# Skip weights on a diagonal per head, added by TensorE, in the scan of a hybrid backbone

## The chip, the cores and the metric

The kernel runs on one core of one Trainium2 chip. The metric is the device time of one launch in microseconds. Three timed runs and one profiled execution of the kernel before are shown below; clocks of TensorE are given as the granted share of full speed (1.00 is 2.4 GHz, 0.50 is 1.2 GHz).

## What is computed

The reference is one inference step of a small backbone: two layers, each applied to 128 context tokens and 1024 latent tokens. A layer norms its input, projects it, and sends parts of the projection to three mixers (attention, a bidirectional state space scan, a convolution module), joins their outputs in an output projection, and ends in a gated feed-forward block. The change is in the scan. Cut to what matters, the reference has:

```python
def ssd_mixer(comb, lp, h0):
    ...
    y = jnp.zeros_like(xs)
    for d in range(2):
        dt = jax.nn.softplus(dt_raw[:, :, d] + lp['ssd_dt_bias'][d])
        a = -jnp.exp(lp['ssd_a_log'][d])
        ...
        yd, hd = ssd_scan(*args, a, h0[:, d])
        ...
        y = y + yd + lp['ssd_d'][d][:, None] * xs
    y = rmsnorm(y.reshape(b, t, SSD_INNER) * jax.nn.silu(z), lp['ssd_norm_g'])
```

`xs` holds 4 heads of 64 values per token. `ssd_scan` works in chunks of 128 tokens: a product inside the chunk (with exponentials of the summed steps) and a product with the state that comes in. The term with `ssd_d` is the skip: each head's inputs times one weight, summed over both directions.

## The kernel before, in words

Tokens are in 9 chunks of 128 (chunk 0 is the context) and in 3 blocks of 384. A layer goes through these stages: projection of the scan's inputs; the mixer stage, where the scan, the projections of the convolution module and of the latents, and the latents' norms run beside each other; attention; output projection; feed-forward. Within the mixer stage generators are stepped through by a string of letters (line 735), so that projections stand between pieces of the scan; the framework then schedules the instructions: it sets the order of each engine's queue by readiness in its own model of the timing, so a change in one place moves neighbours too. Each queue runs strictly in the order thus set.

Values are split in two parts of fp32r ("hi" and "lo") and `mm3` (lines 100 to 105) makes three products of each pair. The projections of the latents from tokens (lines 592 to 614) have 416 columns; they are called projections here, and 24 of them make one tile of 128 tokens.

The scan's output is `ssd_out` (line 474). For a chunk c:

- W holds the step weights of both directions (4 ScalarE products L492, 4 VectorE steps L494), times the chunk's gram matrices (L497 on TensorE, L500 on VectorE).
- Masks for the exponents: for both directions and for hi and lo a tile `mv` of 512 columns, the hi ones by VectorE (L511), the lo ones by four ScalarE products (L509); TensorE multiplies each with a triangle of ones into one bank (L514). Three buffers of `mv`.
- E is the exponential of that (L516) times W (L517).
- TensorE multiplies E with the chunk's inputs, head by head, into `yb`, a bank of tag T (L523). There are eight banks in all: five of tag A, two of tag T, one of tag V.
- VectorE makes y: inputs times `dsum`, the summed skip weights (L525), plus `yb` (L527). From chunk 1 on, the state products of two groups (L532, banks of tag T too) are scaled into `of` (L534), and both directions of `of` are added to y (line 537; the helper's line is 78).
- z times y (L540), its squares summed by ScalarE (L541); every third chunk a norm (L545, L548).

The core of the sum, before:

```python
                y = tmp(256, "y", 2)
                V.tensor_tensor(y.rearrange("p (h q) -> p h q", h=4), xst[:, c].rearrange("p (h q) -> p h q", h=4),
                                dsum.unsqueeze(2).to_broadcast([128, 4, 64]), ALU.mult)
                V.tensor_add(y, y, yb[:, :256])
```

`token_tail` (line 620) norms three latent tiles (L639 to L646) and transposes them (L654, L661) into the latents, which VectorE splits (L581). After the last of these, `prep_r` (line 744) loads rope tables by SP into `tb` (L750) and multiplies them with products (L755); the first scores of attention follow. SP runs its loads in order; ahead of the tables in layer 0 it loads layer 1's rows of weights into a tile that the latents' norm has just read.

Of the kernel before, what the change touches and what calls it, by code (L numbers as in the profile page):

```python
# [9 lines left out]
F32R = mybir.dt.float32r  # L10
I32 = mybir.dt.int32
AF = mybir.ActivationFunctionType
ALU = mybir.AluOpType
# [40 lines left out]
def build(tc, nc, ap, dbg=None):  # L54
    V, S, G, PE, Q = nc.vector, nc.scalar, nc.gpsimd, nc.tensor, nc.sync
# [17 lines left out]
    def bank(tag):  # L73
        n = {"A": 5, "T": 2, "V": 1}[tag]
        return ps.tile([128, 512], F32, tag=tag, name="ps" + tag, bufs=n)

    def add_to(eng, out, a, b):
        eng.tensor_tensor(out, a, b, ALU.add)
# [4 lines left out]
    def copy(out, x):  # L83
        S.activation(out, x, AF.Copy)  # L84
# [47 lines left out]
    ident = cst[:, 0:128]  # L132
# [5 lines left out]
    def P(name, i):  # L138
        return par[:, PAR[name] + i:PAR[name] + i + 1]

    def small(w, tag, bufs=2):
        return sm.tile([128, w], F32, tag=tag, name=tag, bufs=bufs)

    def rsqrt(v, w):
        y = small(w, "ry")
        t = small(w, "rt")
        V.tensor_scalar(y.bitcast(I32), v.bitcast(I32), -0.5, RSQRT_MAGIC, ALU.mult, ALU.add)
        for _ in range(3):
            V.scalar_tensor_tensor(t, y, -0.5, y, ALU.mult, ALU.mult)
            V.tensor_mul(t, t, v)  # L150
            V.scalar_tensor_tensor(y, t, 1.5, y, ALU.add, ALU.mult)
        return y
# [157 lines left out]
    for l in range(L):  # L310
# [62 lines left out]
        def tmp(w, tag, bufs, dt=F32):  # L373
            return w1p.tile([128, w], dt, tag=tag, name=tag, bufs=bufs)


        tmp(512, "mv", 3, F32R)
        tmp(512, "E", 4)

        def xcol(t):  # L380
            return 128 * t + (XP if t else 0)
# [3 lines left out]
        def st_(name, w=72, dt=F32):  # L385
            return w1p.tile([128, w], dt, name=name)
# [20 lines left out]
        def v4(x):  # L407
            return x.rearrange("p (d c h) -> p d c h", d=2, c=9)
# [6 lines left out]
        for i, m in enumerate(M_in + M_st):  # L415
            d = i % 2
# [12 lines left out]
        xst = w1p.tile([128, 9, 256], F32, name="xst")  # L429
# [2 lines left out]
        Q.dma_start(Hin[:, 7, 1], ap["h0"][l, :, 128:256])  # L432
        dsum = st_("dsum", 4)
        V.tensor_add(dsum, rows[:, 16:20], rows[:, 20:24])
        ssz = st_("ssz", 9)


# [36 lines left out]
        def ssd_out():  # L474
            yz, late = [], None

            def tail():
                k, ys = late
                for j in range(2):
                    tb = bank("V")  # L480
                    for t in range(3):
                        PE.transpose(tb[:, 128 * t:128 * t + 128], ys[t][:, 128 * j:128 * j + 128], ident)
                    mo = tmp(CH, "sg", 2)
                    S.activation(mo, tb[:, :CH], AF.Copy, scale=P("ng", 2 * l + j))
                    S.dma_start(m_dram[k][4][:, j], mo)

            for c in range(9):
                o = xcol(c)

                W = tmp(512, "E", 4).rearrange("p (h t) -> p h t", h=4)  # L490
                for h in range(4):
                    S.activation(W[:, h], M_in[0], AF.Copy, scale=v4(dt)[:, 0, c, h:h + 1])  # L492
                for h in range(4):
                    V.scalar_tensor_tensor(W[:, h], M_in[1], v4(dt)[:, 1, c, h:h + 1], W[:, h], ALU.mult, ALU.add)  # L494
                gb = [bank("A"), bank("A")]
                for g in range(2):
                    PE.matmul(gb[g][:, :128], xc[2][64 * g:64 * g + 64, o:o + 128],  # L497
                              xc[3][64 * g:64 * g + 64, o:o + 128], start=True, stop=True)
                for g in range(2):
                    V.tensor_mul(W[:, 2 * g:2 * g + 2], W[:, 2 * g:2 * g + 2],  # L500
                                 gb[g][:, :128].unsqueeze(1).to_broadcast([128, 2, 128]))

                db = bank("A")
                for d in range(2):
                    for i, dd in enumerate((dah, dal)):
                        mv = tmp(512, "mv", 3, F32R).rearrange("p (h t) -> p h t", h=4)
                        if i:
                            for h in range(4):
                                S.activation(mv[:, h], M_in[d], AF.Copy, scale=v4(dd.bitcast(F32))[:, d, c, h:h + 1])  # L509
                        else:  # L510
                            V.tensor_tensor(mv, M_in[d].unsqueeze(1).to_broadcast([128, 4, 128]),  # L511
                                            v4(dd.bitcast(F32))[:, d, c, :].unsqueeze(2).to_broadcast([128, 4, 128]),
                                            ALU.mult)
                        PE.matmul(db, M_sr[d], mv.rearrange("p h t -> p (h t)"), start=d + i == 0, stop=d + i == 2)  # L514
                E = tmp(512, "E", 4).rearrange("p (h t) -> p h t", h=4)
                S.activation(E, db.rearrange("p (h t) -> p h t", h=4), AF.Exp)  # L516
                V.tensor_mul(E, E, W)  # L517
                if late:
                    tail()
                    late = None  # L520
                yb = bank("T")
                for h in range(4):
                    PE.matmul(yb[:, 64 * h:64 * h + 64], E[:, h], xst[:, c, 64 * h:64 * h + 64], start=True, stop=True)  # L523
                y = tmp(256, "y", 2)
                V.tensor_tensor(y.rearrange("p (h q) -> p h q", h=4), xst[:, c].rearrange("p (h q) -> p h q", h=4),  # L525
                                dsum.unsqueeze(2).to_broadcast([128, 4, 64]), ALU.mult)
                V.tensor_add(y, y, yb[:, :256])  # L527
                if c:
                    of = tmp(512, "of", 2).rearrange("p (d h q) -> p d h q", d=2, h=4)
                    for g in range(2):  # L530
                        ob = bank("T")
                        PE.matmul(ob[:, :256], xc[3][64 * g:64 * g + 64, o:o + 128],  # L532
                                  Hin[64 * g:64 * g + 64, c - 1].rearrange("p d n -> p (d n)"), start=True, stop=True)
                        V.tensor_mul(of[:, :, 2 * g:2 * g + 2], ob[:, :256].rearrange("p (d h q) -> p d h q", d=2, h=2),  # L534
                                     v4(ex[:, 0:72])[:, :, c, 2 * g:2 * g + 2].unsqueeze(3).to_broadcast([128, 2, 2, 64]))
                    for d in range(2):
                        add_to(V, y, of[:, d].rearrange("p h q -> p (h q)"), y)
                z = tmp(256, "zr", 4)
                Q.dma_start(z, z_dram[:, c])
                V.tensor_mul(z, z, y)  # L540
                S.activation(y, z, AF.Square, accum_out=ssz[:, c:c + 1])  # L541
                yz.append(z)
                if c % 3 == 2:
                    v = small(3, "nv")
                    V.tensor_scalar(v, ssz[:, c - 2:c + 1], 1.0 / 256, 1e-6, ALU.mult, ALU.add)  # L545
                    r = rsqrt(v, 3)
                    for t in range(3):
                        V.tensor_scalar_mul(yz[t], yz[t], r[:, t:t + 1])  # L548
                    late = (c // 3, yz)
                    yz = []  # L550
                yield
            tail()
# [116 lines left out]
        def step(g, n=1):  # L669
            for _ in range(n):  # L670
                next(g, None)

        st, cv, tm, so = ssd_states(), conv_in(), token_major(), ssd_out()
        gens = {"c": cv, "S": st, "t": tm, "o": so}

# [507 lines left out]
```

## Time and profile before

| | us |
|---|---|
| timed runs | 3262.02, 3253.57, 3265.45 |
| median of these | 3262.02 |
| profiled execution | 3262.04 |
| its span, first to last instruction | 3260.2 |
| busy: TensorE, VectorE, ScalarE, GpSimd | 3118.9, 1770.6, 1145.2, 1069.8 |
| mean granted clock of TensorE | 0.98 |

The mixer stage lies at about 143 to 308 us in layer 0 and 1768 to 1933 us in layer 1. How to read the rows: durations of products on TensorE overlap, so what one costs is the distance from its start to the next start; an arrow in brackets names the time an engine sat idle before an instruction and what ended that. fp32 products are recorded as two each.

### The profile page before, as it was taken

Reading aid. Unit: us, or ns where it says so; the run is one execution under the profiler, and the core shown is the slowest. Engines: PE = TensorE matmul, PEld = TensorE weight load, DVE = VectorE, ACT = ScalarE, POOL = GpSimd, SP = SyncE. Lnnn points to the kernel's source line nnn. Section 1 sums busy time; section 2 is a strip of 40 time slices with the busy share of each in tenths; the row PEclk is TensorE's granted clock in tenths of the full one; section 3 lists DMA queues with packets and bytes.
Section 4 is the critical chain, followed back from the end, with each engine's and each line's share of the span. In section 5 each row is a group of like instructions: output and inputs, shape, how many; then the busy total and the mean of one; then the engine's idle time right before and its main releaser. Section 6 shows DMA issues by size and latency. Waiting matters only on the chain. (4 is left out here: it accounts for less than half of the span.)

```text
span 3260.2 us, 50734 instructions
## 1 busy us (share of the span) xinstructions
PE 3118.9 (96%) x20610; PEld 2898.2 (89%) x20610; DVE 1770.6 (54%) x3891; ACT 1145.2 (35%) x2677; POOL 1069.8 (33%) x601
## 2 busy tenths in 40 slices
PE   7997998999999999999999989999999999999997
PEld 5986777779999999999999867777999999999997
DVE  6768777663633333333386688777373333334335
ACT  4465544562411111111144666566341111111113
POOL 2302998012511221112133039980242221122112
PEclk9998999999999999999999989999999999999998
DMA  6112333342111111111121010001301111111111
GB/s 237 49 31 86 116 118 104 124 171 80 49 42 40 40 51 40 39 40 39 52 103 55 24 58 9 13 6 50 143 27 52 39 52 40 39 42 50 39 33 59
DMA packets 67003, 202.38 MB, mean 62 GB/s; under 512 B 7888, under 2 KB 25424, under 8 KB 65232
## 3 DMA queue, kind: packets, MB, share of 16 engines
q1 hardware_dynamic: 63456, 194.02, 18.0%
q10 hardware_dynamic: 3312, 5.11, 0.4%
q8 instruction: 162, 2.65, 0.3%
q14 instruction: 73, 0.60, 0.1%
HBM read 177.44 MB, written 21.66 MB: 61 GB/s over the span
## 5 line engine op out<-in xcount | busy, mean ns | idle before, releaser
L81 POOL TENSOR_TENSOR wl<-ws,wh 128x1024 fp32r<-128x1024 f32 x164 | 396.0, 2421 | 1611.4 <-ACT wh L84 1571.9
L103 PE MATMUL psA<-hh,wh 128*128 128x384 f32 x2496 | 837.5, 337 | 4.3 <-ACT hh L270 2.7
L104 PE MATMUL psA<-hl,wh 128*128 128x384 f32 x2496 | 838.8, 337 | 1.4 <-DVE hl L267 0.8
L105 PE MATMUL psA<-hh,wl 128*128 128x384 f32 x2496 | 838.3, 336 | 0.0
L103 PEld LDWEIGHTS psA<-hh,wh 128*128 128x128 f32 x2496 | 471.4, 189 | 8.3 <-ACT hh L270 3.9
L104 PEld LDWEIGHTS psA<-hl,wh 128*128 128x128 f32 x2496 | 471.4, 189 | 4.7 <-DVE hl L267 1.7
L105 PEld LDWEIGHTS psA<-hh,wl 128*128 128x128 f32 x2496 | 471.1, 189 | 0.6
L1000 DVE TENSOR_TENSOR fs<-fs,psA 128x384 f32<-128x384 f32 x132 | 72.9, 554 | 666.3 <-PE psA L105 657.3
L873 POOL TENSOR_TENSOR acc<-ct,acc 128x1167 f32<-128x1167 f32 x120 | 326.3, 2719 | 10.0
L84 ACT ACTIVATE wh<-ws 128x1024 fp32r<-128x1024 f32 (+1 forms) x178 | 184.7, 1049 | 401.4 <-PE psA L104 196.3
L999 ACT ACTIVATE fs<-psA 128x384 f32<-128x384 f32 x132 | 63.9, 485 | 655.1 <-PE psA L105 655.0
L810 ACT ACTIVATE P<-psA,mx 128x384 f32<-128x384 f32 (+1 forms) x400 | 224.1, 570 | 128.2 <-DVE mx L808 88.0
L1053 DVE SCALAR_TENSOR_TENSOR x<-psT,mod,x 128x384 f32<-128x384 f32 (+1 forms) x320 | 157.8, 513 | 198.6 <-PE psT L105 198.6
L805 DVE TENSOR_REDUCE mx<-psA 128x1 f32<-128x384 f32 (+1 forms) x400 | 209.3, 540 | 76.5 <-PE psA L105 74.1
L1053 DVE SCALAR_TENSOR_TENSOR x<-psA,mod,x 128x384 f32<-128x384 f32 (+2 forms) x384 | 186.9, 513 | 53.3 <-PE psA L105 46.9
L1003 DVE TENSOR_TENSOR fl<-fs,fh 128x384 fp32r<-128x384 f32 x132 | 167.6, 1271 | 65.9 <-ACT fh L84 65.9
L842 PE MATMUL psV<-pt,vv 128*64 128x128 f32 x2336 | 192.8, 286 | 5.8 <-DVE pt L836 3.9
L831 PE MATMUL psT<-cst,P 128*128 128x128 f32 x1168 | 194.3, 288 | 2.8 <-ACT P L810 1.1
L104 PE MATMUL psA<-fl,wh 128*128 128x384 f32 x576 | 193.6, 336 | 0.0
L105 PE MATMUL psA<-fh,wl 128*128 128x384 f32 x576 | 193.5, 336 | 0.0
L103 PE MATMUL psA<-fh,wh 128*128 128x384 f32 x576 | 190.0, 337 | 2.7 <-DVE fs L1000 2.7
L103 PE MATMUL psA<-K,q 128*128 128x384 f32 (+1 forms) x400 | 159.9, 400 | 29.8 <-ACT P L810 23.7
(265 smaller groups left out, 5884.2 us busy)
## 6 DMA issues: line engine op xcount, KB each, us to landing
ws<-w_ada SPq DMA_DIRECT2D x96, 512.0 KB, 3.3
ws<-w_gate SPq DMA_DIRECT2D x44, 512.0 KB, 3.6
ws<-w_up SPq DMA_DIRECT2D x44, 512.0 KB, 3.6
ws<-w_down SPq DMA_DIRECT2D x44, 512.0 KB, 3.6
x<-xT SPq DMA_DIRECT2D x6, 1536.0 KB, 7.8
ws<-w_fm SPq DMA_DIRECT2D x16, 512.0 KB, 3.5
ws<-w_out SPq DMA_DIRECT2D x16, 512.0 KB, 3.7
mf<-mixed SPq DMA_DIRECT2D x18, 384.0 KB, 5.5
```

Source lines behind the costliest of these rows:

```text
L81: eng.tensor_tensor(out, x, hi.bitcast(F32), ALU.subtract)
L84: S.activation(out, x, AF.Copy)
L103: PE.matmul(out, sh, mh, start=i == 0, stop=False)
L104: PE.matmul(out, sh, ml, start=False, stop=False)
L105: PE.matmul(out, sl, mh, start=False, stop=i == n - 1)
L805: V.reduce_max(mx[:, b:b + 1], b0[:, :w], axis=AX.X)
L810: S.activation(pr[:, CH * b:CH * b + w], bs[b][:, :w], AF.Exp, bias=mx[:, 3:4], scale=SCALE, accum_out=sl[:, 3 * j + b:3 * j + b + 1])
L831: PE.transpose(tb[:, 256 * u + 128 * j:256 * u + 128 * j + 128], prs[j][:, 128 * (a + u):128 * (a + u) + 128], ident)
L842: PE.matmul(ob[64 * j:64 * j + 64, :128], vv[:, kt, 64 * h:64 * h + 64], pt[:, 256 * u + 128 * j:256 * u + 128 * j + 128], start=kt == kts ...
L873: last_tap[0] = G.tensor_tensor(acc[j][:, :CO], ct[:, :CO], acc[j][:, :CO], ALU.add)
L1003: V.tensor_sub(fl[:, sl], sg, fh[:, sl].bitcast(F32))
L1053: V.scalar_tensor_tensor(X[c][:, m, a:b], b0[:, a:b], modT[l][:, 40 + m, s:s + 1], X[c][:, m, a:b], ALU.mult, ALU.add)
```

## The change

Per layer, ScalarE writes four diagonal matrices `dI`, one per head: the identity times that head's summed skip weight. In each chunk TensorE multiplies `dI` with the chunk's inputs into the sum's bank first, and the product with E is added to it there. VectorE's product with `dsum` and the addition of the bank go; the bank is now added to the first direction of `of` (from chunk 1 on), the second direction follows, and in chunk 0 ScalarE copies the bank to y. The tile `mv` has two buffers instead of three; `dI` takes as much memory as one of them.

```diff
-        tmp(512, "mv", 3, F32R)
+        tmp(512, "mv", 2, F32R)
@@
         V.tensor_add(dsum, rows[:, 16:20], rows[:, 20:24])
+        dI = st_("dI", 512).rearrange("p (h t) -> p h t", h=4)
+        for h in range(4):
+            S.activation(dI[:, h], ident, AF.Copy, scale=dsum[:, h:h + 1])
@@
-                        mv = tmp(512, "mv", 3, F32R).rearrange("p (h t) -> p h t", h=4)
+                        mv = tmp(512, "mv", 2, F32R).rearrange("p (h t) -> p h t", h=4)
@@
                 yb = bank("T")
                 for h in range(4):
-                    PE.matmul(yb[:, 64 * h:64 * h + 64], E[:, h], xst[:, c, 64 * h:64 * h + 64], start=True, stop=True)
+                    xh = xst[:, c, 64 * h:64 * h + 64]
+                    PE.matmul(yb[:, 64 * h:64 * h + 64], dI[:, h], xh, start=True, stop=False)
+                    PE.matmul(yb[:, 64 * h:64 * h + 64], E[:, h], xh, start=False, stop=True)
                 y = tmp(256, "y", 2)
-                V.tensor_tensor(y.rearrange("p (h q) -> p h q", h=4), xst[:, c].rearrange("p (h q) -> p h q", h=4),
-                                dsum.unsqueeze(2).to_broadcast([128, 4, 64]), ALU.mult)
-                V.tensor_add(y, y, yb[:, :256])
@@
-                    for d in range(2):
-                        add_to(V, y, of[:, d].rearrange("p h q -> p (h q)"), y)
+                    V.tensor_add(y, of[:, 0].rearrange("p h q -> p (h q)"), yb[:, :256])
+                    add_to(V, y, of[:, 1].rearrange("p h q -> p (h q)"), y)
+                else:
+                    copy(y, yb[:, :256])
```

Lines move by 3 to 4 in the changed kernel: L497, L514, L517, L523 and L532 become L500, L517, L520, L528 and L534 on TensorE and VectorE, and L527 is now the product with `dI`.

The scheduler sets each engine's order anew. TensorE's queue in layer 0 from chunk 5's products with E (`psT<-xst,E`) to its state products (`psT<-Hin,raw_691`), before; `psA<-mv,gtlt` are exponent products, `psA<-raw_691,raw_690` gram products, `128x416` projections:

```order
L523 MATMUL psT<-xst,E 128x64 x4
L514 MATMUL psA<-mv,gtlt 128x512
L105 MATMUL psA<-wh,hl 128x416
L103 MATMUL psA<-wh,hh 128x416
L104 MATMUL psA<-wl,hh 128x416
L105 MATMUL psA<-wh,hl 128x416
L497 MATMUL psA<-raw_691,raw_690 128x128 x2
L514 MATMUL psA<-mv,gtlt 128x512 x2
L532 MATMUL psT<-Hin,raw_691 128x256 x2
```

The same place in the changed kernel, from the last head's two products on:

```order
L527 MATMUL psT<-xst,dI 128x64
L528 MATMUL psT<-xst,E 128x64
L517 MATMUL psA<-mv,gtlt 128x512
L500 MATMUL psA<-raw_691,raw_690 128x128 x2
L517 MATMUL psA<-mv,gtlt 128x512
L534 MATMUL psT<-Hin,raw_691 128x256
L103 MATMUL psA<-wh,hh 128x416
```

One state product now stands there, followed by 24 projections (the first is shown). The other one comes behind these:

```order
L105 MATMUL psA<-wh,hl 128x416
L534 MATMUL psT<-Hin,raw_691 128x256
L517 MATMUL psA<-mv,gtlt 128x512 x2
L103 MATMUL psA<-wh,hh 128x416
L104 MATMUL psA<-wl,hh 128x416
L105 MATMUL psA<-wh,hl 128x416
```

After it come two exponent products and 20 projections, and then chunk 6's products with `dI` and E. Counted from the stage's start, 309 of the three-part products (L103 to L105) stand ahead of chunk 5's products with E before, 313 now.

VectorE's queue at the same place, before (`psT,ex` is the scaling of a state product, `zr<-zr,y` the product with z that ends a chunk):

```order
L527 TENSOR_TENSOR y<-y,psT 128x256
L511 TENSOR_TENSOR mv<-cst,dah 128x512
L525 TENSOR_TENSOR y<-xst,dsum 128x256
L517 TENSOR_TENSOR E<-E 128x512
L494 SCALAR_TENSOR_TENSOR E<-cst,dt,E 128x128 x4
L534 TENSOR_TENSOR of<-psT,ex 128x2x128
L500 TENSOR_TENSOR E<-E,psA 128x256
L534 TENSOR_TENSOR of<-psT,ex 128x2x128
L500 TENSOR_TENSOR E<-E,psA 128x256
L78 TENSOR_TENSOR y<-of,y 128x256 x2
L540 TENSOR_TENSOR zr<-zr,y 128x256
```

And in the changed kernel:

```order
L514 TENSOR_TENSOR mv<-cst,dah 128x512
L520 TENSOR_TENSOR E<-E 128x512
L536 TENSOR_TENSOR of<-psT,ex 128x2x128
L497 SCALAR_TENSOR_TENSOR E<-cst,dt,E 128x128 x4
L503 TENSOR_TENSOR E<-E,psA 128x256 x2
L536 TENSOR_TENSOR of<-psT,ex 128x2x128
L538 TENSOR_TENSOR y<-of,psT 128x256
L78 TENSOR_TENSOR y<-of,y 128x256
L544 TENSOR_TENSOR zr<-zr,y 128x256
L81 TENSOR_TENSOR wl<-ws,wh 128x1024
```

The two scalings of state products stand apart, with chunk 7's weights and gram steps between them; the product with `dsum` and one addition are gone, and the split of a weight (L81) follows, which stood after the chunk's norm before. GpSimd's order is unchanged, ScalarE's and SP's differ in the same stage alone.

## Rows read from the trace of the kernel before

**Rows 1.** The page, its first part: TensorE's busy time, share of the span, instructions.

```profile
PE 3118.9 (96%) x20610; PEld 2898.2 (89%) x20610; DVE 1770.6 (54%) x3891; ACT 1145.2 (35%) x2677; POOL 1069.8 (33%) x601
```

**Rows 2.** Stage windows: busy us of PE, PEld, DVE, ACT, POOL; clock; DMA.

```profile
220.00:240.00 20.00, 20.00 (x109) 16.45 (x108) 16.49 (x63) 12.52 (x44) 0.00 (x0) 1.00 0.09 28
...
260.00:280.00 20.00, 14.41 (x74) 11.40 (x73) 18.19 (x52) 9.76 (x22) 4.91 (x2) 0.85 0.33 115
```

**Rows 3.** Timeline of PE, layer 0: start us, us, instruction [idle before <-releaser].

```profile
215.08 1.00 PE L523 MATMUL psT<-xst,E 128*128 128x64 f32 x8
216.01 0.70 PE L532 MATMUL psT<-Hin,raw 64*128 64x256 f32 x2
...
237.77 0.35 PE L104 MATMUL psA<-wl,hh 128*128 128x416 f32 x1
237.96 0.35 PE L105 MATMUL psA<-wh,hl 128*128 128x416 f32 x1
...
245.94 1.03 PE L514 MATMUL psA<-mv,gtlt 128*128 128x512 f32 x3 [1.62 <-DVE E L500]
...
252.44 1.00 PE L523 MATMUL psT<-xst,E 128*128 128x64 f32 x8
...
254.43 0.49 PE L497 MATMUL psA<-raw,raw 64*128 64x128 f32 x4
254.85 0.74 PE L514 MATMUL psA<-mv,gtlt 128*128 128x512 f32 x2
255.51 0.70 PE L532 MATMUL psT<-Hin,raw 64*128 64x256 f32 x4
```

**Rows 4.** Timeline of DVE, layer 0, chunk 5's sum to chunk 7's.

```profile
253.48 0.42 DVE L527 TENSOR_TENSOR y<-y,psT 128x256 f32<-128x256 f32 x1 [2.05 <-PE psT L523]
253.82 0.69 DVE L511 TENSOR_TENSOR mv<-cst,dah 128x512 fp32r<-128x512 f32 x1
...
257.73 0.88 DVE L78 TENSOR_TENSOR y<-of,y 128x256 f32<-128x256 f32 x2
...
259.65 0.17 DVE L545 TENSOR_SCALAR nv<-ssz 128x3 f32<-128x3 f32 x1 [0.58 <-ACT y L541]
...
261.70 0.42 DVE L527 TENSOR_TENSOR y<-y,psT 128x256 f32<-128x256 f32 x1 [0.51 <-PE psT L523]
...
274.74 0.41 DVE L540 TENSOR_TENSOR zr<-zr,y 128x256 f32<-128x256 f32 x1
275.07 0.87 DVE L78 TENSOR_TENSOR y<-of,y 128x256 f32<-128x256 f32 x2
276.03 0.43 DVE L540 TENSOR_TENSOR zr<-zr,y 128x256 f32<-128x256 f32 x1
```

**Rows 5.** Timelines of SP and of PE, layer 0, where the rope tables come.

```profile
296.19 12.50 SPq L750 DMA_DIRECT2D tb<-rf  x10
...
301.63 0.58 PE L103 MATMUL psA<-wh,lat 128*128 128x256 f32 x1 [3.65 <-DVE tb L755]
```

**Rows 6.** Timeline of PE, layer 1, chunk 5's products with E.

```profile
1877.28 1.00 PE L523 MATMUL psT<-xst,E 128*128 128x64 f32 x8
```

**Rows 7.** Groups by line, DVE, 240 to 300 us: busy us, mean ns.

```profile
L149 DVE SCALAR_TENSOR_TENSOR rt<-ry 128x3 f32<-128x3 f32 (+1 forms) x12 | 1.6, 159 | 0.0
...
L81 DVE TENSOR_TENSOR wl<-ws,wh 128x1024 fp32r<-128x1024 f32 x1 | 1.2, 1219 | 0.0
```

**Rows 8.** Timeline of ACT, layer 0, the first weights of W.

```profile
141.91 1.28 ACT L492 ACTIVATE E<-cst,dt 128x128 f32<-128x128 f32 x4 [4.08 <-DVE dt L402]
```

**Rows 9.** Line L511 (masks on DVE): idle us before it, times, and who ended it.

```profile
  PE psA L514: 8.4, 10
```

**Rows 10.** Timelines of DVE and POOL, layer 0, weight splits on POOL.

```profile
266.58 2.37 DVE L150 TENSOR_TENSOR rt<-rt,v 128x6 f32<-128x6 f32 x1
269.99 2.11 DVE L644 SCALAR_TENSOR_TENSOR tn<-tn,ry,rows 128x128 f32<-128x128 f32 x1
...
266.56 2.37 POOL L81 TENSOR_TENSOR wl<-ws,wh 128x1024 fp32r<-128x1024 f32 x1 [71.52 <-ACT wh L84]
```

## The prediction

> **What bounds the kernel now.** I read the page first. TensorE works through 96% of the span [rows 1], so the question is where it is not full: only there can work taken off VectorE come back as time. The stage windows of layer 0's mixer answer that [rows 2]. From 140 to 240 us TensorE is busy in 20.00 of 20 us (the last of these five windows stands in the rows) at granted clock 1.00, because projections with 416 columns fill every gap of the scan; VectorE waits there. After that the filling thins out: from 260 to 280 us TensorE has 14.41 of 20 us at a clock of 0.85, VectorE 18.19. So a layer's scan has two halves. Chunks 0 to 5 of its nine are paced by TensorE, chunks 6 to 8 and the latents by VectorE; the border is where chunk 5's products with E stand, 252.44 us [rows 3].
>
> The far side ends in a fixed way. VectorE runs almost unbroken from 253.48 us, where it had waited 2.05 us for those products, with waits of 0.58 and 0.51 us, past chunk 7's last product at 276.03 [rows 4], to the end of the latents; behind their last scaling SP issues the loads of the rope tables (296.19), and TensorE goes on at 301.63 after 3.65 us of idleness [rows 5]. What VectorE is late by there, attention is late by. Layer 1 goes through the same two halves, with chunk 5's products at 1877.28 [rows 6]. So each term is worked out for one layer and taken twice. The sum stands against the profiled execution, 3262.04 us (span 3260.2, 1.8 around it); the median of the runs shown is 3262.02, so nothing is to be corrected.
>
> **TensorE: what is added.** Each chunk gets four fp32 products with 64 columns, shaped as the four with E, which are recorded as eight. In the full stretch eight such records go from 215.08 to 216.01, the start of the next [rows 3]: 0.93 us. Eighteen chunks make 16.7 us. Those of chunks 0 to 5 stand where TensorE is full or waited for: 6 x 0.93 = 5.6 us per layer, all on the path. Those of chunks 6 to 8 lie beside VectorE's work and are in the walk below. The order also puts four more projections ahead of chunk 5's products; they start 0.19 us apart (237.77, 237.96 [rows 3]): 0.8 us. Lower bound of the two: TensorE had a wait of its own before chunk 5, 1.62 us at 245.94 [rows 3], that may be taken up, so 4.8 instead of 6.4.
>
> **VectorE: what is taken away.** Two of the four vector steps of a chunk's sum go, the product with dsum and one addition; in a busy stretch such steps start 0.33 us apart (274.74, 275.07 [rows 4]). Before chunk 5 that is worth nothing, as VectorE waits there anyway; if TensorE ceased to be full, 0.67 us per chunk would come back. From 253.48 us on, three products with dsum (chunks 6, 7, 8) and four additions (5 to 8) go: 7 x 0.33 = 2.3 us per layer, all on the path.
>
> **The bank that is held.** The sum's bank is one of the two of tag T, and it is now read only when both state products have been scaled into "of". So the second state product (L532, new L534) can't have the sum's bank any more: it waits until VectorE has scaled the first one out of the only other bank. The order shows it: in chunk 5 the two stood side by side, now 24 projections stand between them. I walk both queues from the end of chunk 5's products. TensorE: exponent product 0.33, gram products 0.42, exponent product 0.33, state product 0.35 (from 254.43, 254.85 and 255.51 [rows 3]), 24 projections 4.6, second state product 0.35: done at 6.4. VectorE: the exponential it needs comes at about 0.6; mask, E, four weights, one half and two gram steps took 3.25 before (253.82 to 257.73 [rows 4], less two other steps of 0.33): at 3.9 it wants the second half, and waits 2.5. Then it has four steps of 0.33, a weight split of 1.2 and nine tiny steps of 0.16 [rows 7] up to chunk 6's first half: at 10.4. TensorE has two exponent products 0.7, 20 projections 3.8, sixteen records for chunk 6 1.9 and a state product 0.35: 13.1. VectorE waits 2.7 more. New waits 5.2, the old ones of 0.58 and 0.51 absorbed: +4.1 per layer. Behind the waiting step stand chunk 7's E and the norm of the latents, so nothing else moves up. Bounds: 0, if VectorE is late anyway and finds the halves ready; 9.2, if two whole batches of 24 projections (4.6 each) fall into such waits. I take the walk's value, which is near the middle.
>
> **What costs nothing.** The four ScalarE products that build dI, once per layer, are like the four that took 1.28 us together, and stand in the 4.08 us of idle ahead of these [rows 8]; without that cover they cost 1.3 us a layer. Chunk 0's sum leaves by ScalarE in the full stretch. Two mask buffers instead of three: VectorE waits for a mask's product to free one for 8.4 us in 10 places over both layers [rows 9], and TensorE has projections meanwhile. I take 0; upper bound, the wait doubles and all of it reaches the path, 8.4 us in the whole. SP gets no new transfer; one weight load and one load of z change places on it, both ahead of the rope tables.
>
> **Sum** per layer: 5.6 + 0.8 - 2.3 + 4.1 = 8.2 us; two layers 16.4. **Forecast 3278.4 us**, 0.5% slower. About 0.5%, 16.3 us, is what a measurement of this kernel can tell from no change, so the forecast lies on that border.
>
> **Rivals.**
> *Columns pace the added products.* A projection of 416 columns takes 0.19 us [rows 3]; by columns a record of 64 takes 0.029 and eight 0.23 instead of 0.93. Then 6 x 0.7 = 4.2 us per layer are saved: 3270. For it: the added products are many and short, and dI is the same in all chunks. Against it: the products with E have their shape and take 0.116 us a record. The same time comes out if chunk 5's old 1.62 and the walk's 2.5 are both covered. The Trainium skill has a rule for the first, in "TensorE: Matmul & The Clock Gate", section "Back-to-back issue gap": a product of 1 to 64 columns occupies some 60 cycles, about 25 ns. By that figure, an estimate, the added products cost 0.2 us a chunk; the 0.116 us a record of this trace disagrees.
>
> *Buffers bind more than the walk says.* The masks' upper bound, 8.4 us, or a second batch of projections inside a wait (4.6 per layer) comes on top: 3287 or 3288; both, 3296. For it: both pools lose a buffer on the engine whose queue orders all others. Against: 20.00 of 20 in the full stretch says that projections cover such waits there.
>
> *Faster: VectorE was what held the stage.* If the tail's idle TensorE time takes in all added products and no new wait arises, these go: 2.3 us of steps, the waits of 1.62, 0.58 and 0.51, and two holds, tiny or 128-column vector steps of 2.37 and 2.11 us, the first as long as the GpSimd step of 2.37 beside it [rows 10]; at 0.16 and 0.35 us, as such steps take otherwise, 4.0 us less. That is 9.0 per layer: 3244. It decides itself at 240 us, where TensorE must be 6.4 us earlier than the full windows let it. Against it, these windows.
>
> *It does next to nothing.* The added products fall into idle TensorE time, and the vector steps were idle time too: 3262. The full windows speak against the first half.
>
> **Chances.** Forecast 0.47 (3270 to 3286, just over half of it beyond 3278.3), columns or fewer waits 0.21, buffers 0.18, faster 0.08, nothing 0.06. Slower by over 0.5%: 0.26 + 0.18 = 0.44. Faster by over 0.5%: 0.08. The rest, 0.48, is within 0.5%. The range runs from 3256 (the "nothing" case less 6 of the 8 us by which the lowest run shown, 3253.57, lies under the median; "faster" is left out) to the buffers' 3296: some 0.12 is left out.
>
> **What would show it.** Right: the window from 220 to 240 us still at 20.00; chunk 5's products near 258 and 1883 us; sixteen records in 1.9 us; VectorE waiting 2 to 3 us for L534 in chunks 5 and 6; TensorE on the rope products, 301.63 before, near 310. Wrong: products with dI at 0.03 us; chunk 5's products no later than before; TensorE waiting for masks; a mixer that ends earlier than before.

## The result, and the profile after

The changed kernel takes 3303.03 us (median of four runs, 3302.74 to 3307.12), the kernel before 3258.83 beside it: a ratio of 1.0132, 95% interval 1.0118 to 1.0145, some 44 us slower. The forecast was 3278.4, a rise of 16.4 us: its sign was right, its size little more than a third of the 44. 3303 lies above the range too, which ended at 3296. The profiled execution has a span of 3300.9 us, 40.7 more than before.

The page of the changed kernel, part 1:

```profile
PE 3155.5 (96%) x20754; PEld 2925.0 (89%) x20754; DVE 1747.5 (53%) x3855; ACT 1146.3 (35%) x2687; POOL 1068.7 (32%) x601
```

Against [rows 1] TensorE has 144 instructions more (18 chunks of eight) and 36.6 us more of busy time, over twice the 16.7 that 144 records take at full speed. So other work takes it longer too. The stage windows of layer 0, columns as in [rows 2]; first one of before that [rows 2] leaves out, then after:

```profile
280.00:300.00 20.00, 16.38 (x86) 13.40 (x84) 16.53 (x64) 13.76 (x40) 0.00 (x0) 0.89 0.16 44
```

```profile
220.00:240.00 20.00, 20.00 (x110) 17.21 (x108) 12.63 (x42) 9.43 (x34) 0.00 (x0) 1.00 0.03 11
...
260.00:280.00 20.00, 18.24 (x104) 15.63 (x102) 14.29 (x35) 11.15 (x31) 4.67 (x2) 1.00 0.15 50
280.00:300.00 20.00, 15.64 (x59) 10.93 (x59) 14.29 (x46) 8.03 (x21) 0.00 (x0) 0.57 0.20 66
```

The full stretch is as full as before. Behind it the picture has turned: VectorE is busy for 14.29 of 20 us where it had 18.19 [rows 2], and from 280 to 300 us TensorE runs at a clock of 0.57, against 0.89 before. Neither engine is full there: they wait for one another. TensorE's timeline of layer 0 after:

```profile
215.86 0.43 PE L527 MATMUL psT<-xst,dI 128*128 128x64 f32 x2
...
217.47 0.39 PE L528 MATMUL psT<-xst,E 128*128 128x64 f32 x2
...
261.23 0.33 PE L527 MATMUL psT<-xst,dI 128*128 128x64 f32 x2
...
264.18 0.70 PE L534 MATMUL psT<-Hin,raw 64*128 64x256 f32 x2
264.81 0.46 PE L103 MATMUL psA<-wh,hh 128*128 128x416 f32 x1
...
269.27 0.35 PE L105 MATMUL psA<-wh,hl 128*128 128x416 f32 x1
269.56 0.70 PE L534 MATMUL psT<-Hin,raw 64*128 64x256 f32 x2
...
276.36 0.70 PE L534 MATMUL psT<-Hin,raw 64*128 64x256 f32 x2
...
280.93 1.22 PE L534 MATMUL psT<-Hin,raw 64*128 64x256 f32 x2 [2.69 <-DVE of L536]
...
283.05 0.69 PE L527 MATMUL psT<-xst,dI 128*128 128x64 f32 x2
...
287.18 1.22 PE L534 MATMUL psT<-Hin,raw 64*128 64x256 f32 x2
```

Chunk 5's products stand at 261.23 instead of 252.44 [rows 3]. Its two state products lie 5.4 us apart, with the 24 projections between them. Chunk 6's second half waits 2.69 us for the bank. TensorE is then at half clock: chunk 7's sixteen records and one batch of transposes among them take from 283.05 to 287.18, where chunk 2's sixteen took from 215.86 to about 217.8. VectorE's timeline of the same stretch:

```profile
265.50 0.42 DVE L536 TENSOR_TENSOR of<-psT,ex 128x256 f32<-128x256 f32 x1
...
270.29 0.43 DVE L536 TENSOR_TENSOR of<-psT,ex 128x256 f32<-128x256 f32 x1 [2.66 <-PE psT L534]
...
273.39 1.23 DVE L81 TENSOR_TENSOR wl<-ws,wh 128x1024 fp32r<-128x1024 f32 x1 [1.30 <-ACT wh L84]
...
275.13 2.32 DVE L150 TENSOR_TENSOR rt<-rt,nv 128x3 f32<-128x3 f32 x1
277.48 2.28 DVE L151 SCALAR_TENSOR_TENSOR ry<-rt,ry 128x3 f32<-128x3 f32 x1
...
280.46 0.42 DVE L536 TENSOR_TENSOR of<-psT,ex 128x256 f32<-128x256 f32 x1
...
288.44 0.42 DVE L536 TENSOR_TENSOR of<-psT,ex 128x256 f32<-128x256 f32 x1 [2.38 <-PE psT L534]
...
307.57 0.42 DVE L536 TENSOR_TENSOR of<-psT,ex 128x256 f32<-128x256 f32 x1 [3.36 <-PE psT L534]
```

In chunks 5, 7 and 8 VectorE waits for a state product. In chunk 6 it is TensorE that waits: ahead of VectorE's first scaling there stand a wait of 1.30 us for ScalarE and two norm steps of 2.3 us on three columns, which run beside two weight splits on GpSimd:

```profile
275.07 4.67 POOL L81 TENSOR_TENSOR wl<-ws,wh 128x1024 fp32r<-128x1024 f32 x2 [78.43 <-ACT wh L84]
```

Such holds were there before too [rows 10]; now the first scaling, and behind it the bank, and behind that TensorE, wait for them. The end of the stage, timelines of SP and of PE after:

```profile
316.71 8.40 SPq L754 DMA_DIRECT2D tb<-rf  x5
```

```profile
322.12 0.58 PE L103 MATMUL psA<-wh,lat 128*128 128x256 f32 x1 [2.50 <-DVE tb L759]
```

Against [rows 5] both are 20.5 us later. Of these 8.8 had come by chunk 5's products and 11.7 arise behind them. The same place in layer 1, before and after:

```profile
1925.63 0.58 PE L103 MATMUL psA<-wh,lat 128*128 128x256 f32 x1 [1.62 <-DVE tb L755]
```

```profile
1971.79 0.58 PE L103 MATMUL psA<-wh,lat 128*128 128x256 f32 x1 [1.61 <-DVE tb L759]
```

It is 46.2 us later, so layer 1 loses another 25.7; 5.5 us are given back behind it.

### The profile page after: what moved, and what is told of

Read it like the earlier page. It is cut to its first block, busy times and chain, and to the rows that moved or that the text cites. A ratio compares the mean times of both kernels' runs of the same rounds, so it can differ in the third digit from the quotient of the medians.

```text
span 3300.9 us, 50978 instructions
## 1 busy us (share of the span) xinstructions
PE 3155.5 (96%) x20754; PEld 2925.0 (89%) x20754; DVE 1747.5 (53%) x3855; ACT 1146.3 (35%) x2687; POOL 1068.7 (32%) x601
## 5 line engine op out<-in xcount | busy, mean ns | idle before, releaser
L81 POOL TENSOR_TENSOR wl<-ws,wh 128x1024 fp32r<-128x1024 f32 x164 | 395.3, 2418 | 1619.6 <-ACT wh L84 1579.9
L103 PE MATMUL psA<-hh,wh 128*128 128x384 f32 x2496 | 835.8, 337 | 4.4 <-ACT hh L270 2.7
L105 PE MATMUL psA<-hh,wl 128*128 128x384 f32 x2496 | 836.7, 336 | 0.0
L103 PEld LDWEIGHTS psA<-hh,wh 128*128 128x128 f32 x2496 | 470.1, 189 | 8.3 <-ACT hh L270 3.9
L105 PEld LDWEIGHTS psA<-hh,wl 128*128 128x128 f32 x2496 | 470.0, 188 | 0.4
L105 PE MATMUL psA<-fh,wl 128*128 128x384 f32 x576 | 193.8, 336 | 0.0
L103 PE MATMUL psA<-fh,wh 128*128 128x384 f32 x576 | 190.2, 337 | 2.7 <-DVE fs L1004 2.7
L103 PE MATMUL psA<-K,q 128*128 128x384 f32 (+1 forms) x400 | 159.0, 397 | 26.0 <-ACT P L814 19.8
```

Source lines behind the costliest of these rows:

```text
L81: eng.tensor_tensor(out, x, hi.bitcast(F32), ALU.subtract)
L103: PE.matmul(out, sh, mh, start=i == 0, stop=False)
L105: PE.matmul(out, sl, mh, start=False, stop=i == n - 1)
```

## The experiments

Eighteen kernels ran. Each is told as the difference in us of its median to that of the kernel before on the same chip, with the ratio and its interval (3 to 6 us to either side).

**First set: the parts.** e1 is before with two mask buffers (the other line that names mv likewise):

```diff
-        tmp(512, "mv", 3, F32R)
+        tmp(512, "mv", 2, F32R)
```

> The kernel before with one edit: two buffers of mv instead of three. Theory 'bank hold' (the 44 us come from the sum's bank being read only behind both scalings): masks are worth little, 0 to +8 us, as the prediction bounded them. Rival 'masks' (the lost buffer couples VectorE, ScalarE and TensorE more tightly): most of the loss is here, +25 to +44 us. Rival 'many small ones': +8 to +20 us.

Measured: +2 (1.0006, 0.9997 to 1.0015). Over the whole kernel the masks alone are nearly free. In the profiled execution the mixer of layer 0 still ends 6.4 us later than before (TensorE's first rope product at 308.05 us instead of 301.63); layer 1 and what follows give it back.

e2 is the changed kernel with three:

```diff
-        tmp(512, "mv", 2, F32R)
+        tmp(512, "mv", 3, F32R)
...
-        dI = st_("dI", 512).rearrange("p (h t) -> p h t", h=4)
-        for h in range(4):
-            S.activation(dI[:, h], ident, AF.Copy, scale=dsum[:, h:h + 1])
...
-                    PE.matmul(yb[:, 64 * h:64 * h + 64], dI[:, h], xh, start=True, stop=False)
+                    PE.matmul(yb[:, 64 * h:64 * h + 64], ident, xh, start=True, stop=False)
```

> The changed kernel with three buffers of mv again; as there is no memory for dI beside them, the identity stands in its place as TensorE's operand (the sum gets the inputs once, not times the skip weights), and its four ScalarE products per layer go. Bank hold: still +35 to +44 us over the kernel before. Masks: +5 to +17 us (what the products cost). Many small ones: +22 to +36 us.

Measured: +34 (1.0110, 1.0090 to 1.0129), inside the range of many small ones and just under the hold's. Beside the rest of the change the third buffer is worth 10 us, which e1 did not show.

e3 is the changed kernel with the bank copied out at once by ScalarE:

```diff
+                copy(y, yb[:, :256])
                 if c:
...
-                    V.tensor_add(y, of[:, 0].rearrange("p h q -> p (h q)"), yb[:, :256])
-                    add_to(V, y, of[:, 1].rearrange("p h q -> p (h q)"), y)
-                else:
-                    copy(y, yb[:, :256])
+                    for d in range(2):
+                        add_to(V, y, of[:, d].rearrange("p h q -> p (h q)"), y)
```

> The changed kernel, but ScalarE copies the sum's bank to y in every chunk as in chunk 0, so that the bank is free before the state products, and VectorE adds both directions of 'of' to y. Same VectorE steps as the changed kernel, same products, two mask buffers, no hold. Bank hold: down to +5 to +12 us over the kernel before (added products less two vector steps a chunk). Masks: still +30 to +44 us. Many small ones: +15 to +30 us.

Measured: +24.5 (1.0070, 1.0056 to 1.0084). More came back than the masks theory allows, less than the hold theory wanted; many small ones had the range.

e4 should have held the bank in the kernel before:

```diff
-                V.tensor_add(y, y, yb[:, :256])
...
+                    V.tensor_add(y, y, yb[:, :256])
                     for d in range(2):
...
+                else:
+                    V.tensor_add(y, y, yb[:, :256])
```

> The kernel before with one edit: the addition of the sum's bank to y stands behind both scalings of the state products (from chunk 1 on), so that the bank is held as in the changed kernel; all vector steps, three mask buffers and no added products. Bank hold: +25 to +40 us. Masks: +8 us, what the prediction's walk gave for the hold (4.1 per layer). Many small ones: +10 to +22 us.

Measured: -3 (0.9990, 0.9981 to 0.9999). The run does not test what it was made for. The addition depends on the bank alone, and the scheduler put it back ahead of the scalings, as VectorE's timeline of e4 in chunk 5 shows:

```profile
252.67 0.42 DVE L535 TENSOR_TENSOR y<-y,psT 128x256 f32<-128x256 f32 x1 [0.46 <-PE psT L523]
...
255.60 0.41 DVE L533 TENSOR_TENSOR of<-psT,ex 128x256 f32<-128x256 f32 x1
```

**Second set: products, and the hold undone or left alone.** e5 is before with the added products only:

```diff
-                    PE.matmul(yb[:, 64 * h:64 * h + 64], E[:, h], xst[:, c, 64 * h:64 * h + 64], start=True, stop=True)
+                    xh = xst[:, c, 64 * h:64 * h + 64]
+                    PE.matmul(yb[:, 64 * h:64 * h + 64], ident, xh, start=True, stop=False)
+                    PE.matmul(yb[:, 64 * h:64 * h + 64], E[:, h], xh, start=False, stop=True)
```

> The kernel before with one edit: ahead of each product with E, TensorE multiplies the identity with the same inputs into the same place of the bank (the sum gets the inputs once more); every vector step, three mask buffers, no hold. Theory 'products are dearer than their time': +20 us or more. Rival 'they cost what they take' (5.6 per layer in the full stretch, at most 8.4): +11 to +17 us. Rival 'covered by idle TensorE time': 0 to +6 us.

Measured: +6 (1.0017, 1.0006 to 1.0029), at the border of the last of the three.

e7 is the changed kernel without them:

```diff
-                    PE.matmul(yb[:, 64 * h:64 * h + 64], dI[:, h], xh, start=True, stop=False)
-                    PE.matmul(yb[:, 64 * h:64 * h + 64], E[:, h], xh, start=False, stop=True)
+                    PE.matmul(yb[:, 64 * h:64 * h + 64], E[:, h], xh, start=True, stop=True)
```

> The changed kernel without TensorE's products with dI (the skip is left out of the sum): two mask buffers, the held bank, two vector steps less a chunk. Theory 'products are dearer than their time': -8 to 0 us against the kernel before. Rival 'the hold costs once VectorE has fewer steps to do in the meantime': +10 to +25 us. Theory 'they cost what they take': +27 to +33 us, the changed kernel's +44 less 11 to 17.

Measured: +28 (1.0083, 1.0070 to 1.0096), inside the last range. So most of the loss is there without any added product.

e9 is the changed kernel with the sum in tag V:

```diff
-                yb = bank("T")
+                yb = bank("V")
```

> The changed kernel with the sum in the bank of tag V (otherwise used by the transposes that follow every third chunk), so that both banks of tag T are free for the two state products; the sum is held as before, but nothing of the same chunk waits for it. If the serialised state products make the loss: +5 to +15 us over the kernel before, below the early copy's +24.5. If the added products make it: +24 to +40 us. If the transposes in V then wait for the sum: as much as the changed kernel, +44.

Measured: +20 (1.0055, 1.0037 to 1.0073), between the first two ranges.

e6 is before with the skip on ScalarE:

```diff
-                V.tensor_tensor(y.rearrange("p (h q) -> p h q", h=4), xst[:, c].rearrange("p (h q) -> p h q", h=4),
-                                dsum.unsqueeze(2).to_broadcast([128, 4, 64]), ALU.mult)
+                for h in range(4):
+                    S.activation(y[:, 64 * h:64 * h + 64], xst[:, c, 64 * h:64 * h + 64], AF.Copy, scale=dsum[:, h:h + 1])
```

> The kernel before with the skip as four ScalarE products of 64 columns per chunk in place of VectorE's product with dsum: one vector step less a chunk, nothing added on TensorE, no hold, three mask buffers. If VectorE's steps pace the second half: -2 to -6 us. If ScalarE's copies behind them are paced too: 0 to +5 us.

Measured: +6 (1.0014, 1.0005 to 1.0022), just above the second range. A vector step less brings nothing here, though TensorE gets no product for it; ScalarE gets four.

**Third set: the hold made binding.** e10 is before with

```diff
-                V.tensor_add(y, y, yb[:, :256])
...
+                    V.tensor_add(of[:, 0], of[:, 0], yb[:, :256].rearrange("p (h q) -> p h q", h=4))
                     for d in range(2):
...
+                else:
+                    V.tensor_add(y, y, yb[:, :256])
```

> The kernel before with the hold made binding: the sum's bank is added onto the first direction of 'of' in place, so that it can be read only behind both scalings; VectorE keeps its four steps a chunk (the product with dsum among them), three mask buffers, nothing added on TensorE. Theory 'hold' (the bank kept through both scalings makes most of the loss): +15 to +25 us. Rival 'fewer vector steps shuffle the order' (it is the steps taken out, not the hold): -3 to +5 us. The prediction's walk: +8 us.

Measured: +30 (1.0091, 1.0078 to 1.0104), with all vector steps, three buffers and no product more: the hold, and more of it than its theory had.

e11 has two buffers besides (the diffs of e10 and e1 together):

> The same with two mask buffers. Theory 'hold', with buffers that add up: 0 to +10 us on top of the run with three. Theory 'hold and masks bind only together': +22 to +30 us here, under +8 with three. Rival 'fewer vector steps': 0 to +7 us here.

Measured: +33 (1.0103, 1.0090 to 1.0116), 3 more than with three buffers, as the first theory had it.

e12 is e3 with the copy on VectorE (`V.tensor_copy(y, yb[:, :256])`):

> The changed kernel (products with dI, two mask buffers), but VectorE copies the sum's bank to y at once and then adds both directions of 'of': no hold, three vector steps a chunk. Theory 'hold': +8 to +14 us over the kernel before (what the products and the masks cost alone, 6 and 2, and a little). Rival 'fewer vector steps': +20 to +30 us, as with the early copy by ScalarE.

Measured: +27 (1.0084, 1.0071 to 1.0097), as the rival had it. e13 is e5 with the product with dsum left out and the addition of the bank turned into the same copy:

> The run of the products alone (+6 us) less VectorE's product with dsum: VectorE copies the sum's bank (identity and E) to y, then adds both directions of 'of'; three mask buffers, no hold. Theory 'hold': 0 to +6 us. Rival 'fewer vector steps': +12 to +25 us.

Measured: +15 (1.0050, 1.0036 to 1.0063), as the rival had it too. Both cost some 8 us more than the kernels from which they differ by the copy in place of product and addition (e13 against e5; e12 against e14 below, which also has the identity in the place of dI). VectorE waits 17.5 us for the sum in 12 places at e12's copy and 7.2 in 9 at e14's addition, but 3.7 in 6 at e13's copy and at e5's addition alike. So that wait does not explain the 8 us, and they stay open.

**Fourth set.** e14 is e5 and e1 together; e15 is e2 with the sum in tag V; e16 is e10 with the sum in tag V; e17 is e7 with three mask buffers and no dI.

> The kernel before with the added products (identity times inputs) and two mask buffers, all vector steps, no hold. If the two costs add up: +6 to +10 us. If the lost mask buffer binds once TensorE has less idle time to give (an interaction): +15 to +25 us.

Measured: +19.5 (1.0059, 1.0045 to 1.0072): 6 and 2 make 19.5, an interaction.

> The changed kernel with the sum in the bank of tag V, three mask buffers, and the identity in the place of dI (there is no memory for both): added products and fewer vector steps remain. If the masks interact with the products: +5 to +12 us over the kernel before, against +20 with two mask buffers. If the masks are worth little: +16 to +22 us.

Measured: +39 (1.0119, 1.0103 to 1.0134), 19 more than e9, which has a buffer less. Neither theory has that, and it stays open.

> The forced hold (+30 us) with the sum in the bank of tag V: it is read as late as there, but the state products have both banks of tag T. Theory 'the second state product waits for the bank': -3 to +6 us. Rival 'late reading itself, or the order that it brings': +20 to +30 us.

Measured: +26 (1.0086, 1.0071 to 1.0100), as the rival had it. TensorE waits before no state product for a scaling there. There is one bank of tag V, and the products with E wait for it only briefly, for the read of the chunk before (L535) and for ScalarE's of the transposes (L484); whole span, us, times, longest:

```profile
PE psV L523 <- DVE of L535: 1.4, 4, 0.5
PE psV L523 <- ACT sg L484: 0.5, 2, 0.2
```

But the order has moved with the bank. Three chunks' products with E stand close together in layer 0, and the next come 39 us later:

```profile
245.79 1.55 PE L523 MATMUL psV<-xst,E 128*128 128x64 f32 x8 [0.21 <-DVE of L535]
...
284.72 1.97 PE L523 MATMUL psV<-xst,E 128*128 128x64 f32 x8 [0.24 <-ACT sg L484]
```

So a late read costs as much where no second state product waits for it, in an order of its own. How much of the hold's price in tag T is that wait, and how much the order that a late read brings, is not separated. Tag V gives back 24 us in e9 and 4 in e16 and costs 5 more in e15 (against e2): these runs decide no more than that.

> The changed kernel without products with dI (the skip is left out) and with three mask buffers: the hold and two vector steps less a chunk remain. Theory 'hold': +18 to +30 us, the forced hold's 30 less what the vector steps are worth. If two mask buffers made the +28 of the run without products: under +10 us.

Measured: +29.5 (1.0088, 1.0075 to 1.0102): the hold's price, with two masks or three (e7, e17) and with all vector steps or two less (e10, e17).

**Last set: the hold undone with all the change's work kept.** e18 is the changed kernel with the block of the state products and their scalings moved ahead of the sum:

```diff
+                if c:
+                    of = tmp(512, "of", 2).rearrange("p (d h q) -> p d h q", d=2, h=4)
...
                 yb = bank("T")
                 for h in range(4):
...
                 if c:
-                    of = tmp(512, "of", 2).rearrange("p (d h q) -> p d h q", d=2, h=4)
...
                     V.tensor_add(y, of[:, 0].rearrange("p h q -> p (h q)"), yb[:, :256])
```

> The changed kernel with the state products and their scalings written ahead of the products with dI and E; the sum's bank is then read as soon as it is full. Same work on every engine, two mask buffers. Theory 'hold costs about 28, products with two mask buffers about 19': +14 to +22 us over the kernel before. Rival 'it is the order that the scheduler makes of fewer vector steps': +25 us or more.

Measured: +16 (1.0052, 1.0034 to 1.0070): 28 of the 44 us are gone, with two vector steps less still in it.

e19 does that to the kernel before, with `V.tensor_add(y, y, yb[:, :256])` as the chunk's last addition:

> The kernel before with the same order: state products, their scalings and both additions ahead of the sum, one vector step left behind it; three mask buffers, nothing added. If VectorE's steps behind the products with E pace the second half: -2 to -8 us. If the tag's two banks then make the sum wait for a scaling: +5 to +20 us. No difference: -2 to +2 us.

Measured: +7 (1.0024, 1.0013 to 1.0035), in the second range. No version beats the kernel before by more than e4's 0.1%.

**What the sets say together.** Eight kernels make a full table of three parts (us over before; the hold comes with two vector steps less in its rows):

| | three masks | two masks |
|---|---|---|
| neither | 0 | +2 (e1) |
| products | +6 (e5) | +19.5 (e14) |
| hold | +29.5 (e17) | +28 (e7) |
| hold and products | +34 (e2) | +44 (changed kernel) |

The hold costs 25 to 30 us in each of its four pairs. The products cost 5 or 6 us with three buffers and 16 or 17 with two. Two buffers cost 2 or -2 us without products and 10 or 13 beside them. Each edit also brings an order of its own, and edits that give TensorE no work cost 6 to 8 us (e6, e19, the copies): the hold's price is well above that, the products' 5 or 6 is not.

What the hold does is read at VectorE's waits ahead of the scalings (whole span: us, times): before, e10, the changed kernel, e18.

```profile
  PE psT L532: 8.7, 5
```

```profile
  PE psT L531: 22.3, 17
```

```profile
  PE psT L534: 39.7, 19
```

```profile
  PE psT L528: 17.5, 16
```

TensorE's waits for a scaling ahead of the state products (us, times, longest) are none before and 6.0 to 7.3 us in the six kernels with the hold in tag T; e10, the changed kernel and e18:

```profile
PE psT L531 <- DVE of L533: 6.3, 4, 2.6
```

```profile
PE psT L534 <- DVE of L536: 6.4, 4, 2.7
```

```profile
PE psT L528 <- DVE of L530: 1.0, 2, 0.5
```

What it costs TensorE in layer 0 stands in one window from 150 us to VectorE's first rope product, again before, e5, e14, e10, e18, the changed kernel:

```profile
150.00:301.00 151.00, 138.79 (x755) 117.32 (x753) 103.45 (x327) 89.70 (x254) 14.59 (x14) 0.95 0.14 44
```

```profile
150.00:305.60 155.60, 148.07 (x830) 125.60 (x829) 102.64 (x328) 90.27 (x254) 15.91 (x14) 0.96 0.14 43
```

```profile
150.00:308.90 158.90, 146.40 (x829) 124.36 (x827) 102.07 (x329) 89.96 (x254) 14.77 (x14) 0.97 0.14 42
```

```profile
150.00:314.20 164.20, 148.88 (x762) 122.95 (x760) 102.98 (x328) 91.20 (x256) 15.54 (x14) 0.90 0.13 39
```

```profile
150.00:310.30 160.30, 146.92 (x825) 123.67 (x823) 98.94 (x311) 88.91 (x255) 14.12 (x13) 0.96 0.14 42
```

```profile
150.00:321.50 171.50, 154.87 (x827) 128.44 (x825) 100.18 (x310) 89.44 (x255) 14.19 (x14) 0.92 0.13 38
```

Length less busy time is idleness; length times (1 less the clock) is what the clock takes, good to 0.8 us as the clock has two digits. Before: 12.2 and 7.6 us. With the forced hold: 15.3 and 16.4, so 3.1 and 8.8 of its 13.2 us. Changed kernel against e18, the same work with and without the hold: 3.2 and 7.3 of 11.2 us. Busy time says the same without the clock: for the same products TensorE is busy 10.1 us longer with the forced hold than before, and 8.0 longer in the changed kernel than in e18. Over the whole span the profiled executions have a granted clock of 0.971 to 0.977 in the six kernels with the hold in tag T, 0.980 before and 0.983 in e18. In these windows the larger part of the hold's price is not the time for which TensorE stands still, but the time for which it runs at 1.2 GHz, whose stretches lie behind such waits (280.93 above). That order was seen, not tested: no run kept the clock up through a wait. The products alone (e5) have 7.5 us of idleness, 4.7 less than before: they fill idle time.

The masks' interaction was looked for in the waits of TensorE's exponent products (whole span: us, times, longest). Before has one kind, e5 none:

```profile
PE psA L514 <- DVE E L500: 3.2, 2, 1.6
```

With two buffers, e1 and e14:

```profile
PE psA L514 <- ACT mv L509: 3.2, 2, 1.6
PE psA L514 <- DVE mv L511: 2.5, 3, 1.1
```

```profile
PE psA L514 <- ACT mv L509: 5.0, 4, 2.0
PE psA L514 <- DVE mv L511: 2.3, 2, 1.1
```

With three buffers TensorE never waits for a mask; with two it does, for 5.7 us in e1 and 7.3 in e14. In e1 these waits stand in the place of the 3.2 us of before. The added products of e5 live on idle time, of which 7.5 us are left in layer 0; in e14 it is 12.5 us again. That masks and products contend for it fits the table; it is not shown. e18 has products and two buffers too and lies at +16 with 2.3 us of such waits, so they are no measure of the interaction.

## Why the prediction was wrong in size

**TensorE, what is added** (forecast 6.4 per layer with the four projections, 12.8 in all). The price of a record was right: sixteen take 1.9 us. One of the five windows that it took for full was not quite: TensorE is busy in 19.65 of 20 us from 160 to 180 us. With three buffers the products alone cost 5 or 6, so part of them fell into TensorE's idle time; with the change's two buffers 16 or 17. Both sides of the forecast occur; the condition that decides was not in it.

**VectorE, what is taken away** (forecast -2.3 per layer). Worth 0 to -2.5 per layer behind a hold (e10 against e17, e11 against e7); without a hold a step less brought nothing (e6, e13).

**The bank that is held** (forecast +4.1 per layer): the step that failed, 8.2 us in all against 25 to 30 measured. The wait that it named is in the trace, and the first half of the walk came out: VectorE's wait in chunk 5 is 2.66 us where the walk had 2.5. The second wait changed sides. The walk gave the nine norm steps 0.16 us each; two of them took 2.3 beside GpSimd, and VectorE waited 1.30 for ScalarE ahead of the weight split, so VectorE was late and TensorE waited 2.69 instead. The walk ended there, and two things lay behind its end: the waits of chunks 7 and 8 (2.38 and 3.36), and TensorE's fall to half clock, which the walk priced nowhere though [rows 2] showed 0.85 in this very stage. Its upper bound, 9.2 per layer, was too low for the same reasons. And it took the wait for the whole price, where e16 shows one as high without it; what the order that a late read brings is worth stays open. Ahead of the walk chunk 5 already started 8.8 us later where the sum had 6.4; 1.8 us of TensorE's waits for masks lie there.

**What costs nothing.** Two buffers: forecast 0, upper bound 8.4. Alone they cost 2, as said; beside the products 10 to 13, above the bound. The sum took each edit by itself and added; that products and masks are dear together was not in it. The prediction had named TensorE waiting for masks as a sign of its being wrong, and the sign is there (2.3 us for VectorE's, 1.4 for ScalarE's in the changed kernel).

By the measured parts the sum comes out nearly: hold with fewer vector steps 29.5 (e17), products 6, masks 2, and 11 that products and masks cost together beyond these: 49 against 44.

**Rivals.** Buffers binding more came nearest, with its sign and both its places right; its 3296 is 7 us short, and it too added waits at full clock. Columns as the pace fell: the Trainium skill, "TensorE: Matmul & The Clock Gate", "Back-to-back issue gap", gives about 25 ns to products of up to 64 columns; here, as fp32 products, they take 0.12 us a record. Faster, and nothing, are out: the mixer ends 20.5 us later in layer 0.

## What to carry to other kernels

Adding a term in the accumulator saves vector steps, but look at who reads the accumulator last: a bank that is read only when another result has come is held for that long, and it brings another order of the queues. Compute that other result first: here that gave 28 of 44 us back. Test edits together, and not only each alone: a buffer less and a few more products were cheap each (2 and 6 us) and dear together (19.5). And price a wait of TensorE with the clock that follows it, not by its length alone.

## What was not expected of the hardware

The low clock took about 8.8 us in layer 0 with the forced hold where idleness took 3.1. Two vector steps on three columns took 2.32 and 2.28 us beside GpSimd's splits one after the other; in the kernel before, the two holds of layer 0 lay apart [rows 10]. That two or three mask buffers turn the sum in tag V from +20 to +39, with the third buffer the slower one, stays open; so do the 8 us of the copies.
